# Ends of an attention and FFN trunk on one core: where norm weights load, how the last products are cut, who multiplies last

## The chip, the cores and the metric

The kernel runs on one core of one Trainium2 chip. The metric is the device time of one execution in microseconds (us); less is better. The kernel before was timed three times, with a median of 1301.2 us.

## The reference

Two decoder layers on 512 tokens of width 1024, then a last RMSNorm. The first layer mixes with stick-breaking and native sparse attention, the second with forgetting attention; each ends with a gated MLP that has a causal depthwise convolution on one branch. Cut to what the change touches:

```python
def rmsnorm(x, g):
    x32 = x.astype(jnp.float32)
    y = x32 * lax.rsqrt(jnp.mean(x32 * x32, axis=-1, keepdims=True) + NORM_EPS)
    return y.astype(x.dtype) * g

def conv_glu_ffn(h, w_in, conv_w, conv_b, w_out):
    a, b = jnp.split(h @ w_in, 2, axis=-1)
    a = conv(a, conv_w) + conv_b              # causal, depthwise, width 3
    return (jax.nn.silu(a) * b) @ w_out

def reference(x, ...):
    for layer in range(DEPTH):                # 2
        h = rmsnorm(x, attn_norm[layer])
        x = x + mixer(h)                      # even or odd layer
        x = x + conv_glu_ffn(rmsnorm(x, ffn_norm[layer]), ...)
    return rmsnorm(x, final_norm)
```

## The kernel before

Everything is kept transposed: the residual x is eight chunks X[0] to X[7] of 128 channels (partitions) by 512 tokens, two chunks to a tile. A product with a weight matrix is made in float32 accuracy from three products of rounded halves: high weight by high input, low weight by high input, high weight by low input. So each input chunk is held as a pair (xh, xl, made by scale_x), and each weight block, 128x1024 numbers for eight chunks, is loaded as wraw on the SP queue, cast to whi on ScalarE (L193) and subtracted to wlo on VectorE (L194). wraw, whi and wlo have two buffers each. The norm weights g are folded into xh and xl (tile ng); the division by the root of the mean square is made later, on the results, with the vector rstd. The mean square needs the sum of the squares of all eight chunks (ACC, by squares), a product with ones on TensorE (norm_stats), and inv_sqrt: one step on VectorE, two on ScalarE (logarithm and exponential), three on VectorE.

Work for TensorE is written as generators. unit is one block of 24 products of 512 columns into one PSUM bank, with a use that evacuates it; vgroup makes the values in four token blocks (tb 0 to 3); proj is an output projection that adds into X[m]. A queue, Fill, runs them in order and starts the next one (its weight load) when its predecessor begins: `_start(2)`. In the attention stages pipeline interleaves them with the attention of head pairs.

A scheduler of the framework puts the instructions of each engine into a fixed order, mostly that of the program, with an eye to when operands will be ready. Each engine then runs its list in order; the order rows below show that list.

Start of the program (layer0). The SP queue loads the first weight block in four pieces, then six of the eight x chunks, further weights and constants. The ScalarE queue loads x chunks 0 and 2, and then ng (L569). TensorE runs eight products of zeros (warm) to be busy before there is work. The constant mask32 takes one of the two buffers that the squares use, and maskb is made from it on GpSimd (L166); the third square (chunk 2) waits for that. Four units follow in the queue (here U0, U4, U1, U5: blocks 0, 4, 1, 5 of the first input projection), then a vgroup. Only `_start(2)` is called ahead of the squares, so U1's cast and subtraction stand behind the norm's first step in the lists.

Start of layer 1. The queue holds unit U[0] and a vgroup. U[0] and the token blocks of the vgroup take the two "mm" banks of PSUM in turn; U[0]'s bank is free when q is evacuated (L335), for which rstd must be there.

End of the program (ffn with final, then finish). Eleven blocks of the last projection (GH, GL) make each X[m]. Chunks 0 to 6 go through proj: 33 products of 512 columns, an addition to X[m] (L476), a square on ScalarE, a sum on GpSimd (L239), and a multiplication of X[m] with its norm weight on ScalarE (L931). The last chunk, m = 7, goes through finish, in two token parts of 320 and 192 columns: its 33 products for each part (a call of products), square (addition L291, square L293), the product with ones, and out, which runs inv_sqrt, multiplies all chunks by rstd and stores them with four DMAs. Of the eight multiplications of a part, VectorE makes four (L301) and the one of chunk 7 with its norm weight (L302), GpSimd makes three (chunks 1, 3, 5). The program calls out(0) before square(1).

Of the kernel before, what the change touches and what calls it, by code (L numbers as in the profile page):

```python
# [9 lines left out]
F32 = mybir.dt.float32  # L10
F32R = mybir.dt.float32r
BF = mybir.dt.bfloat16
AF = mybir.ActivationFunctionType
ALU = mybir.AluOpType
# [3 lines left out]
P = 128  # L18
# [86 lines left out]
def trunk(ctx, tc, A):  # L105
# [62 lines left out]
    def warm():  # L168

        z = cp.tile([P, SEQ], BF, name="zero")  # L170
        pool.memset(z, 0.0)
        ps = pp.tile([P, SEQ], F32, tag="t", bufs=1, name="t")
        for n in range(8):
            mm(ps, z[:, 0:P], z, n == 0, n == 7)
# [91 lines left out]
    def finish(srcs, oh, ol):  # L266

        n = len(oh)
        m = NK - 1
        ws = [weights(src, [P, kn, P]) for src, kn in srcs]  # L270
        hw = [(h[:, k], l[:, k]) for (h, l), (_, kn) in zip(ws, srcs) for k in range(kn)]
        parts = (slice(0, 320), slice(320, SEQ))
        st = s_banks()
        pss, sqs = [], []

        def products(b, ks):
            t = parts[b]
            w = t.stop - t.start
            if b == len(pss):
                pss.append(pp.tile([P, SEQ], F32, tag="mm", bufs=2, name="mm"))  # L280
            ps = pss[b][:, 0:w]
            for k in ks:
                h, l = hw[k]
                mm(ps, h, oh[k][:, t], k == 0, False)
                mm(ps, l, oh[k][:, t], False, False)
                mm(ps, h, ol[k][:, t], False, k == n - 1)

        def square(b):
            t = parts[b]
            w = t.stop - t.start  # L290
            dve.tensor_add(X[m][:, t], X[m][:, t], pss[b][:, 0:w])  # L291
            sq = wp.tile([P, SEQ], F32, tag="sq2", bufs=2, name="sq")
            act.activation(sq[:, 0:w], X[m][:, t], AF.Square)  # L293
            sqs.append(sq[:, 0:w])

        def out(b):
            t = parts[b]
            w = t.stop - t.start
            inv_sqrt(rstd[:, t], st[:, b, 0:w], w)
            for c in (0, 2, 1, 4, 3, 6, 5):  # L300
                (pool if c in (1, 3, 5) else dve).tensor_mul(X[c][:, t], X[c][:, t], rstd[:, t])  # L301
            dve.scalar_tensor_tensor(X[m][:, t], X[m][:, t], ng[:, 4, m:m + 1], rstd[:, t], op0=ALU.mult, op1=ALU.mult)  # L302
            for c in range(0, NK, 2):
# [725 lines left out]
```

## Time and profile before

| what | us |
|---|---|
| timed runs | 1303.6, 1301.2, 1296.93 |
| median | 1301.2 |
| the profiled execution | 1299.13 |
| its span on the core | 1297.4 |
| TensorE busy in it | 1269.5 |
| VectorE, ScalarE, GpSimd busy | 694.5, 557.4, 155.1 |
| bytes moved by DMA | 124.00 MB |

The span is what the views of the trace show, from the first instruction to the end; 1.7 us lie around it. Times of rows count from the span's start. A row of the timeline gives start, duration, engine, line of the program, operation and tiles (written <- read), shape and count, and in brackets how long the engine sat idle before and what released it. Products overlap on TensorE, so a duration is longer than the distance to the next start; the distances are what a stream costs. The granted clock of TensorE is given in full speed: 1.00 is 2.4 GHz and 0.50 is 1.2 GHz.

### The profile page before, as it was taken

The page shows a single profiled execution, that of the slowest core. Times are in us where ns is not written, and L with a number is a line of the kernel's source. Part 1 is how long each engine was busy: PE and PEld are TensorE (multiplying, and loading weights), DVE is VectorE, ACT ScalarE, POOL GpSimd, SP SyncE. Part 2 cuts the span into 40 slices and gives each one's busy share as a digit, 9 for nine tenths or more (in the row PEclk, how much of TensorE's full clock was granted, in tenths as well). Part 3 has the DMA queues.
Part 4 walks back from the last instruction along what each step waited for, and adds up shares of the span by engine and source line. Part 5 has one row for each costly group of instructions (what it writes and reads, how often), then busy time and mean ns, then how long its engine had stood idle before and what let it go on. Part 6 is the DMA issues. An engine that isn't in the chain of part 4 may idle for free.

```text
span 1297.4 us, 16449 instructions
## 1 busy us (share of the span) xinstructions
PE 1269.5 (98%) x6297; PEld 1000.7 (77%) x6297; DVE 694.5 (54%) x1135; ACT 557.4 (43%) x948; POOL 155.1 (12%) x213
## 2 busy tenths in 40 slices
PE   8999999999999999999999999999999999999995
PEld 5876856567888888888887877776788888888884
DVE  7468665538655435555453453344755533555534
ACT  6466465645433223334342554444533322333332
POOL 1000032223000000000111433321200000000012
PEclk9999999999999999999999999999999999999997
DMA  6325201003333233232344453411332233333232
GB/s 216 90 65 151 77 29 43 19 25 123 98 98 94 80 103 113 99 97 78 92 129 144 140 146 100 118 43 57 116 97 97 88 91 113 98 98 98 83 95 83
DMA packets 50640, 124.00 MB, mean 96 GB/s; under 512 B 6321, under 2 KB 15793, under 8 KB 50561
## 3 DMA queue, kind: packets, MB, share of 16 engines
q1 hardware_dynamic: 49040, 121.35, 31.0%
q10 hardware_dynamic: 1520, 1.59, 0.4%
q8 instruction: 50, 0.82, 0.3%
q14 instruction: 30, 0.24, 0.1%
HBM read 119.28 MB, written 2.13 MB: 94 GB/s over the span
## 4 chain that ended last, share of the span: by engine, by line
PE 94%; DVE 3%; DMA 1%; ACT 1%; issue 1%; POOL 0%; DVEq 0%; ACTq 0%
PE mm L115 80%; PE s L115 6%; PE o L115 4%; PE t L412 4%; DMA x<-x 1%; DMA mask<-mask 0%; DVE x L301 0%; DVE e L449 0%; DMA wc<-wcv 0%; DVE acc L239 0%; DVE lt L444 0%; DVE wlo L194 0%; ACT lt L441 0%; ACT whi L193 0%; DVE e L450 0%
## 5 line engine op out<-in xcount | busy, mean ns | idle before, releaser
L115 PE MATMUL mm<-xh,whi 128*128 128x512 f32 x944 | 375.8, 398 | 2.4 <-ACT xh L248 2.1
L193 ACT CAST whi<-wraw 128x1024 fp32r<-128x1024 f32 (+2 forms) x221 | 201.6, 913 | 392.7 <-PE mm L115 373.7
L115 PE MATMUL mm<-xl,whi 128*128 128x512 f32 x944 | 369.4, 391 | 0.1
L115 PE MATMUL mm<-xh,wlo 128*128 128x512 f32 x944 | 368.5, 390 | 0.8 <-DVE wlo L194 0.8
L194 DVE TENSOR_TENSOR wlo<-wraw,whi 128x1024 fp32r<-128x1024 f32 (+2 forms) x221 | 236.8, 1072 | 143.0 <-ACT whi L193 140.1
L115 PEld LDWEIGHTS mm<-xh,whi 128*128 128x128 f32 x944 | 177.8, 188 | 46.8 <-issue 9.1
L115 PEld LDWEIGHTS mm<-xl,whi 128*128 128x128 f32 x944 | 177.6, 188 | 39.0 <-issue 1.0
L115 PEld LDWEIGHTS mm<-xh,wlo 128*128 128x128 f32 x944 | 177.9, 188 | 37.0 <-DVE wlo L194 1.5
L115 PE MATMUL mm<-gh,whi 128*128 128x512 f32 (+2 forms) x363 | 139.3, 384 | 0.0
L115 PE MATMUL mm<-gh,wlo 128*128 128x512 f32 (+2 forms) x363 | 139.1, 383 | 0.0
L115 PE MATMUL mm<-gl,whi 128*128 128x512 f32 (+2 forms) x363 | 139.1, 383 | 0.0
L403 POOL TENSOR_SCALAR e<-e,dn 128x512 f32<-128x512 f32 (+3 forms) x128 | 77.4, 625 | 177.3 <-DVE dn L397 91.4
L390 ACT ACTIVATE e<-e,nm 128x512 f32<-128x512 f32 (+3 forms) x128 | 70.4, 551 | 49.4 <-DVE nm L388 49.4
L413 ACT COPY ph<-t 128x512 f32<-128x512 f32 x100 | 58.2, 582 | 70.3 <-PE t L412 70.2
L237 POOL COPY acc<-sq 128x512 f32<-128x512 f32 x4 | 2.8, 707 | 651.4 <-ACT sq L234 651.4
L769 DVE TENSOR_TENSOR a<-mm,rstd 128x512 f32<-128x512 f32 x44 | 30.4, 692 | 92.1 <-PE mm L115 91.9
L476 DVE TENSOR_TENSOR x<-x,mm 128x512 f32<-128x512 f32 x63 | 43.2, 686 | 67.3 <-PE mm L115 67.0
L115 PEld LDWEIGHTS mm<-gh,wlo 128*128 128x128 f32 x363 | 68.2, 188 | 13.5
L115 PEld LDWEIGHTS mm<-gh,whi 128*128 128x128 f32 x363 | 68.2, 188 | 13.4
L115 PEld LDWEIGHTS mm<-gl,whi 128*128 128x128 f32 x363 | 68.2, 188 | 13.2
L777 DVE TENSOR_TENSOR b<-mm,rstd 128x512 f32<-128x512 f32 x44 | 30.4, 692 | 72.4 <-PE mm L115 72.3
L773 ACT ACTIVATE tt<-tt 128x512 f32<-128x512 f32 x44 | 27.8, 632 | 86.8 <-DVE tt L772 86.8
(160 smaller groups left out, 1603.0 us busy)
## 6 DMA issues: line engine op xcount, KB each, us to landing
wraw<-wfi SPq DMA_DIRECT2D x88, 512.0 KB
wraw<-wu SPq DMA_DIRECT2D x31, 512.0 KB
wraw<-wfo SPq DMA_DIRECT2D x32, 384.0 KB
wraw<-wfo SPq DMA_DIRECT2D x32, 320.0 KB
wraw<-wo SPq DMA_DIRECT2D x32, 256.0 KB
cb<-cd SPq DMA_DIRECT2D x8, 512.0 KB
x<-x SPq DMA_DIRECT2D x14, 256.0 KB
wraw<-wv SPq DMA_DIRECT2D x6, 528.0 KB
```

Of the source, the lines that this page charges most:

```text
L115: pe.matmul(out, l, r, start=st, stop=sp_)
L193: act.copy(h, w)
L194: dve.tensor_sub(l, w, h.bitcast(F32))
L237: eng.tensor_copy(ACC[0], sq)
L390: act.activation(ei, ei, AF.Exp, bias=nm, scale=-1.0, accum_out=dn)
L403: pool.tensor_scalar(ei, ei, self.dn[:, hd, i:i + 1], 1.0, op0=ALU.mult, op1=ALU.mult)
L412: pe.transpose(ps[:, o:o + P], self.e[:, hd, EOFF[i] + j * P:EOFF[i] + j * P + P], ident)
L413: act.copy(self.ph[:, 512 * n:512 * n + 512], ps)
L476: dve.tensor_add(X[m], X[m], ps)
L769: dve.tensor_mul(a, ps, rstd)
L773: silu.append(act.activation(t, t, AF.Silu).ins)
L777: dve.tensor_mul(b, ps, rstd)
```

## The change

Four places are edited. At the start, the load of ng is issued first on the ScalarE queue, ahead of x chunks 0 and 2; warm runs 12 products of zeros in place of 8; and `fl._start(3)` is called ahead of norm_stats, so that U1's weights are loaded, cast and subtracted earlier in the lists. In layer 1, unit U[0] writes to an "s" bank of PSUM in place of an "mm" bank. At the end, finish now takes chunks 6 and 7, both in two token parts; the weights of chunk 6 get tiles of their own (fh, fl); the multiplications are all on VectorE; and the additions of the second part stand in its list ahead of the last multiplications of the first.

```diff
@@ warm
-        for n in range(8):
-            mm(ps, z[:, 0:P], z, n == 0, n == 7)
+        for n in range(12):
+            mm(ps, z[:, 0:P], z, n == 0, n == 11)
@@ finish
-    def finish(srcs, oh, ol):
+    def finish(fp, src, oh, ol):
         n = len(oh)
-        m = NK - 1
-        ws = [weights(src, [P, kn, P]) for src, kn in srcs]
-        hw = [(h[:, k], l[:, k]) for (h, l), (_, kn) in zip(ws, srcs) for k in range(kn)]
+        ms = (NK - 2, NK - 1)
+        hw = {}
+        for m in ms:
+            own = lambda sh: tuple(fp.tile(sh, F32R, tag=f"{t}{sh[1]}", bufs=1, name=t) for t in ("fh", "fl"))
+            ws = [(weights(a, [P, kn, P], own if m == ms[0] else None), kn) for a, kn in src(m)]
+            hw[m] = [(h[:, k], l[:, k]) for (h, l), kn in ws for k in range(kn)]
         parts = (slice(0, 320), slice(320, SEQ))
+        width = (320, 192)
         st = s_banks()
...
+        def square(m, b, ps):
+            t, w = parts[b], width[b]
+            added.append(dve.tensor_add(X[m][:, t], X[m][:, t], ps[:, 0:w]).ins)
+            sq = wp.tile([P, SEQ], F32, tag="sq2", bufs=4, name="sq")
+            act.activation(sq[:, 0:w], X[m][:, t], AF.Square)
+            return sq[:, 0:w]
+
+        def scale(b, cs):
             t = parts[b]
...
-            for c in (0, 2, 1, 4, 3, 6, 5):
-                (pool if c in (1, 3, 5) else dve).tensor_mul(X[c][:, t], X[c][:, t], rstd[:, t])
-            dve.scalar_tensor_tensor(X[m][:, t], X[m][:, t], ng[:, 4, m:m + 1], rstd[:, t], op0=ALU.mult, op1=ALU.mult)
-            for c in range(0, NK, 2):
-                (act if c in (0, 4) else sp).dma_start(A["out"][c:c + 2, :, t].rearrange("c p s -> p c s"), XX[c // 2][:, :, t])
+            for c in cs:
+                if c in ms:
+                    dve.scalar_tensor_tensor(X[c][:, t], X[c][:, t], ng[:, 4, c:c + 1], rstd[:, t], op0=ALU.mult, op1=ALU.mult)
+                else:
+                    dve.tensor_mul(X[c][:, t], X[c][:, t], rstd[:, t])
+                if c % 2 == 1:
+                    (act if c in (1, 5) else sp).dma_start(A["out"][c - 1:c + 1, :, t].rearrange("c p s -> p c s"), XX[c // 2][:, :, t])
...
+        sqs = {}
+        added = []
         for b in range(2):
+            for m in ms:
+                ps = pp.tile([P, SEQ], F32, tag="mm", bufs=2, name="mm")
+                if (m, b) == (ms[0], 1):
+                    products(m, b, ps, range(4))
+                    for m2 in ms:
+                        mm(st[:, 0, 0:320], ones, sqs[m2, 0], False, m2 == ms[1])
+                    inv_sqrt(rstd[:, parts[0]], st[:, 0, 0:320], 320)
+                    products(m, b, ps, range(4, n))
+                else:
+                    products(m, b, ps, range(n))
+                if (m, b) == (ms[1], 1):
+                    scale(0, range(5))
+                sqs[m, b] = square(m, b, ps)
+                if (m, b) == (ms[0], 0):
+                    for b2 in range(2):
+                        mm(st[:, b2, 0:width[b2]], ones, ACC[0][:, parts[b2]], True, False)
+        with tc.issue_after(added[-1]):
+            for m2 in ms:
+                mm(st[:, 1, 0:192], ones, sqs[m2, 1], False, m2 == ms[1])
+            inv_sqrt(rstd[:, parts[1]], st[:, 1, 0:192], 192)
+            scale(0, range(5, NK))
+            scale(1, range(NK))
@@ layer0
             h, l, w = weights(U[0], [P, NK, P], pieces=4)
+            act.dma_start(ng, A["ng"])
             load_x(True)
-            act.dma_start(ng, A["ng"])
...
             fl.step(NK - 1)
+            fl._start(3)
             norm_stats(True)
@@ ffn
-                    fl.add(*[proj(m, src(m), GH, GL, use) for m in range(NK - 1)])
+                    fl.add(*[proj(m, src(m), GH, GL, use) for m in range(NK - 2)])
                     fl.all()
-                    finish(src(NK - 1), GH, GL)
+                    finish(fp, src, GH, GL)
@@ layer1
-            fl.add(unit(U[0], q_use(0)), vgroup(wv(0), 272, v_use(0), (v_l1, None)), unit(U[8], k_use(0)),
+            fl.add(unit(U[0], q_use(0), s_bank), vgroup(wv(0), 272, v_use(0), (v_l1, None)), unit(U[8], k_use(0)),
```

VectorE's list at the start, from the first sum of squares (acc) to the norm's steps (rs_t, rs_u, rstd), in the kernel before. The first wlo is U4's, the two behind rs_t are U1's and U5's:

```order
L237 COPY acc<-sq 128x512
L194 TENSOR_TENSOR wlo<-wraw,whi 128x1024
L239 TENSOR_TENSOR acc<-acc,sq 128x512 x7
L259 TENSOR_SCALAR rs_t<-s 128x512
L194 TENSOR_TENSOR wlo<-wraw,whi 128x1024 x2
```

The same stretch of VectorE's list in the changed kernel:

```order
L237 COPY acc<-sq 128x512
L194 TENSOR_TENSOR wlo<-wraw,whi 128x1024
L239 TENSOR_TENSOR acc<-acc,sq 128x512 x5
L194 TENSOR_TENSOR wlo<-wraw,whi 128x1024
L239 TENSOR_TENSOR acc<-acc,sq 128x512 x2
L259 TENSOR_SCALAR rs_t<-s 128x512
```

U1's subtraction has moved ahead of the norm's first step, and stands between the fifth and the sixth of seven additions; on ScalarE its cast stands likewise ahead of the last two squares.

VectorE's list at the end, in the kernel before: from rstd of the first part to the addition of chunk 7's second part (x_1489, x_1492, x_1495 and x_1498 are the tiles of chunks 0 and 1, 2 and 3, 4 and 5, 6 and 7):

```order
L264 SCALAR_TENSOR_TENSOR rstd<-rs_u,rstd 128x320
L301 TENSOR_TENSOR x_1489<-x_1489,rstd 128x320
L301 TENSOR_TENSOR x_1492<-x_1492,rstd 128x320
L301 TENSOR_TENSOR x_1495<-x_1495,rstd 128x320
L301 TENSOR_TENSOR x_1498<-x_1498,rstd 128x320
L302 SCALAR_TENSOR_TENSOR x_1498<-x_1498,ng,rstd 128x320
L291 TENSOR_TENSOR x_1498<-x_1498,mm 128x192
L259 TENSOR_SCALAR rs_t<-s 128x192
```

The same in the changed kernel, where these tiles are x_1493, x_1496, x_1499 and x_1502:

```order
L264 SCALAR_TENSOR_TENSOR rstd<-rs_u,rstd 128x320
L301 TENSOR_TENSOR x_1493<-x_1493,rstd 128x320 x2
L301 TENSOR_TENSOR x_1496<-x_1496,rstd 128x320 x2
L301 TENSOR_TENSOR x_1499<-x_1499,rstd 128x320
L290 TENSOR_TENSOR x_1502<-x_1502,mm 128x192 x2
L301 TENSOR_TENSOR x_1499<-x_1499,rstd 128x320
L299 SCALAR_TENSOR_TENSOR x_1502<-x_1502,ng,rstd 128x320 x2
L259 TENSOR_SCALAR rs_t<-s 128x192
```

All eight multiplications are now in this list; the two additions of the second part (chunks 6 and 7) stand behind five of them, and three stand behind the additions. Outside the start and the end the lists of all engines are the same in both kernels, but for the PSUM bank of U[0] in layer 1.

## Rows read from the trace of the kernel before

**Rows 1.** The page: busy us, share of the span and instructions by engine.
```profile
PE 1269.5 (98%) x6297; PEld 1000.7 (77%) x6297; DVE 694.5 (54%) x1135; ACT 557.4 (43%) x948; POOL 155.1 (12%) x213
```

**Rows 2.** TensorE's waits: total us, times, longest.
```profile
PE s L115 <- ACT sq L293: 5.9, 1, 5.9
...
PE s L115 <- DVE wlo L194: 1.5, 1, 1.5
...
PE mm L115 <- DVE q L335: 1.2, 1, 1.2
```

**Rows 3.** Timeline, start of the program, all engines, to TensorE's fifth block.
```profile
5.96 2.98 ACT L248 ACTIVATE xh<-x,ng 128x512 fp32r<-128x512 f32 x4 [0.75 <-DMA ng<-ng]
...
13.70 1.23 DVE L194 TENSOR_TENSOR wlo<-wraw,whi 128x1024 fp32r<-128x1024 f32 x1 [0.25 <-ACT whi L193]
13.73 1.66 POOL L166 CAST maskb<-mask 128x512 bf16<-128x512 f32 x1 [11.56 <-DMA mask<-mask]
...
14.98 0.50 PE L115 MATMUL mm<-xh,wlo 128*128 128x512 f32 x1 [0.39 <-DVE wlo L194]
...
16.09 4.67 DVE L239 TENSOR_TENSOR acc<-acc,sq 128x512 f32<-128x512 f32 x6 [0.15 <-ACT sq L234]
...
20.81 1.13 PE L115 MATMUL s<-acc,ones 128*128 128x512 f32 x2 [0.56 <-DVE acc L239]
...
22.01 0.39 PE L115 MATMUL s<-xh,whi 128*128 128x512 f32 x1
...
23.91 0.50 PE L115 MATMUL s<-xh,wlo 128*128 128x512 f32 x1 [1.52 <-DVE wlo L194]
```

**Rows 4.** Stretches at the start: busy by engine, granted clock, DMA share, GB/s.
```profile
6.00:8.00 2.00, 1.22 (x3) 0.79 (x4) 1.21 (x2) 1.89 (x3) 0.00 (x0) 0.87 0.88 301
8.00:10.00 2.00, 2.00 (x6) 1.52 (x6) 1.99 (x4) 1.86 (x5) 0.00 (x0) 0.50 1.00 369
```

**Rows 5.** Timeline, start of layer 1, the vgroup's first two token blocks.
```profile
681.14 0.29 PE L115 MATMUL mm<-whi,xl 128*128 128x272 f32 x1
...
682.65 0.39 PE L115 MATMUL mm<-vhi,xh 128*128 128x272 f32 x1 [1.22 <-DVE q L335]
...
683.58 0.46 ACT L341 ACTIVATE vt<-mm,rtok 128x256 f32<-128x256 f32 x1
```

**Rows 6.** Timeline, end of the program, first products of each piece of chunks 6 and 7.
```profile
1264.55 0.39 PE L115 MATMUL mm<-gh,whi 128*128 128x512 f32 x1
...
1272.03 0.30 PE L115 MATMUL mm<-gh,whi 128*128 128x320 f32 x1
...
1276.86 0.25 PE L115 MATMUL mm<-gh,whi 128*128 128x192 f32 x1
...
1278.18 1.05 PE L115 MATMUL s<-acc,ones 128*128 128x320 f32 x4
1279.06 0.70 PE L115 MATMUL s<-sq,ones 128*128 128x320 f32 x2
```

**Rows 7.** Timeline, end of the program, from rstd of the first part.
```profile
1282.64 0.49 DVE L264 SCALAR_TENSOR_TENSOR rstd<-rs_u,rstd 128x320 f32<-128x320 f32 x1
1283.17 3.68 DVE L301 TENSOR_TENSOR x<-x,rstd 128x320 f32<-128x320 f32 x4
1286.78 0.54 DVE L302 SCALAR_TENSOR_TENSOR x<-x,ng,rstd 128x320 f32<-128x320 f32 x1
1287.24 0.34 DVE L291 TENSOR_TENSOR x<-x,mm 128x192 f32<-128x192 f32 x1
...
1288.03 1.01 PE L115 MATMUL s<-sq,ones 128*128 128x192 f32 x2 [5.95 <-ACT sq L293]
1289.08 0.36 DVE L259 TENSOR_SCALAR rs_t<-s 128x192 f32<-128x192 f32 x1 [1.50 <-PE s L115]
...
1291.50 2.34 DVE L301 TENSOR_TENSOR x<-x,rstd 128x192 f32<-128x192 f32 x4
...
1293.77 0.41 DVE L302 SCALAR_TENSOR_TENSOR x<-x,ng,rstd 128x192 f32<-128x192 f32 x1
```

More of the change, by code (lines that the diff above doesn't have):

```diff
@@ L272, in finish @@
         parts = (slice(0, 320), slice(320, SEQ))
+        width = (320, 192)
         st = s_banks()
-        pss, sqs = [], []
-        def products(b, ks):
-            t = parts[b]
[L278 to L299, printed above, removed]
-            for c in (0, 2, 1, 4, 3, 6, 5):
-                (pool if c in (1, 3, 5) else dve).tensor_mul(X[c][:, t], X[c][:, t], rstd[:, t])
-            dve.scalar_tensor_tensor(X[m][:, t], X[m][:, t], ng[:, 4, m:m + 1], rstd[:, t], op0=ALU.mult, op1=ALU.mult)
-            for c in range(0, NK, 2):
-                (act if c in (0, 4) else sp).dma_start(A["out"][c:c + 2, :, t].rearrange("c p s -> p c s"), XX[c // 2][:, :, t])
@@ L306, in finish, with products @@
-        products(0, range(n))
-        square(0)
-        products(1, range(4))
-        for b in range(2):
-            mm(st[:, b, 0:parts[b].stop - parts[b].start], ones, ACC[0][:, parts[b]], True, False)
-        mm(st[:, 0, 0:320], ones, sqs[0], False, True)
-        products(1, range(4, n))
-        out(0)
-        square(1)
-        mm(st[:, 1, 0:192], ones, sqs[1], False, True)
-        out(1)
+        def products(m, b, ps, ks):
+            for k in ks:
+                h, l = hw[m][k]
+                o, t = ps[:, 0:width[b]], parts[b]
+                mm(o, h, oh[k][:, t], k == 0, False)
+                mm(o, l, oh[k][:, t], False, False)
+                mm(o, h, ol[k][:, t], False, k == n - 1)
```

## The prediction

> **What bounds the kernel now.** TensorE is busy for 98% of the span [rows 1], so I read first its waits [rows 2]: what is not a wait of TensorE, or work after its last product, is hidden. Four waits lie where the change is made: 5.9 us at the very end for a square, 1.5 us at the start for U1's wlo, 1.2 us in layer 1 for q; the fourth is the sum of squares at the start, 0.56 us [rows 3]. Then I read the three places in order of time, to see for each what the waiting instruction's own engine did until then [rows 3 to 7]. Between these places the lists of instructions are the same, so I take a gain at the start to be carried to the end.
>
> **The start.** In the trace the sum of squares is the path: GpSimd gets the mask at 13.73 and frees a buffer of the squares 1.66 us later, the additions run from 16.09 in steps of 0.79 (six end at 20.76), and the product with ones starts at 20.81, which I call S [rows 3]. TensorE was not late for it: U4's second product had to wait until 14.98 for its wlo (13.70 and 1.23 us), and 23 products of 0.227 us (the distance in [rows 6], 7.48 us for 33) end by 20.2.
>
> That decides two edits. ng's load, ahead of the x chunks, lets ScalarE begin earlier than 5.96, where it sat idle 0.75 us for ng, and 12 products of zeros keep TensorE busy until then; the granted clock was 0.87 and 0.50 from 6 to 10 us [rows 3, 4]. Both speed up U0 alone, up to some 1.5 us of it, and behind U0 the product waits for U4's wlo all the same: I cost them at nothing, by cover of that wait. One side effect counts: on the SP queue the second x load waits for the first load of the ScalarE queue to land, which was x chunk 0 and is now the small ng. DMA moved 301 GB/s from 6 to 8 us against 369 after that [rows 4]; if the hole closes, 2 us x 68/369 = 0.4 us are won for all that follows in the queue, the mask among them. The price of the move itself, x chunk 0 issued one load later, is bounded by the 0.75 us that ScalarE waited for ng, and hidden there.
>
> `_start(3)` moves U1's cast ahead of the last two squares on ScalarE and its subtraction between the fifth and sixth addition on VectorE. The addition behind it waits, and behind that the product with ones: 1.23 us [rows 3], and I take 0.15 us for the hand-over and give back 0.2, since the last two squares are then ready (0.70 a step, not 0.79): 1.2 us. So S goes to 20.81 + 1.2 - 0.4 = 21.6. What it buys: before, U1's second product came at 23.91, 3.10 us after S. Now its wlo is there, and what remains is the product with ones and one more product, which took 22.01 - 20.81 = 1.20 us. 3.10 - 1.20 - (1.2 - 0.4) = **1.1 us** won. Bounds: if the mask comes no earlier and TensorE's idle time ahead of S (20.2 to 22.0) brings the clock down as it was from 8 to 10 us [rows 4], some 3 us at half speed cost 1.5 us: 0.7 - 1.5 = -0.8. If the subtraction fits into a gap and S stays early: 1.9 + 0.4 = 2.3.
>
> **Layer 1.** U[0] held one of two "mm" banks until q was evacuated. The last product of the vgroup's first token block began at 681.14, the next block's first at 682.65 [rows 5]; by the columns a product costs 0.227 x 272/512 = 0.12, so the hole is **1.4 us**. With U[0] in an "s" bank the second block starts at once. What is late next: the third block takes the first one's bank, which ScalarE frees at 683.58 + 0.46 = 684.04; the second block, 24 products, would end at 681.26 + 2.9 = 684.2. The cover is 0.15 us; whatever is missing there is lost one to one, so 0.9 is the lower bound. The norm's own "s" bank is another one.
>
> **The end, TensorE.** Chunk 6 starts at 1264.55 [rows 6]. 33 products of 320 columns took 4.83 us (1272.03 to 1276.86), 12 of 192 took 1.32, so 33 take 3.63: together 8.46 against 7.48 in one piece. The cut costs 1.0 us, and the products with ones that are added, 0.5 (part one, by the distance from 1279.06) and 0.3. In the new order: 1264.55 + 4.83 + 0.88 (sum, 1278.18 to 1279.06) + 4.83 + 1.32 + 1.06 + 2.31 + 3.63 = 1283.4 for the last product; before it was 1288.03 - 5.95 = 1282.1 [rows 7].
>
> By the Trainium skill (TensorE: Matmul & The Clock Gate, section "Back-to-back issue gap"), an isolated product of N columns costs N/2.4 + 2.5 ns, 136, 82 and 216 ns for 320, 192 and 512, so that the cut would cost 0.1 us, not 1.0, and the time below would be 1293.8. The rows show 146, 110 and 227 ns for these streams, and I go by them.
>
> **The end, VectorE.** Before, the second part's addition (1287.24) stood behind five multiplications of the first [rows 7], 5.2 us after the last product. Now part one's products with ones end at 1264.55 + 12.92 = 1277.5, 2.1 us earlier than before (1279.6), so its rstd is ready at 1283.13 - 2.1 = 1281.0. The price of a multiplication on VectorE alone isn't in the trace: 3.68/4 = 0.92 us for 320 columns with GpSimd at work beside it, 0.49 for another operation of that shape (L264), and 0.46 from the start of L302 to that of the addition behind it. I take 0.46 (nearest: same tiles, same engine), and 0.33 for 192 columns (0.36 for rs_t, less the same overlap; with GpSimd beside it 2.34/4 = 0.59). Five end at 1283.3, so the addition waits for TensorE, not for them: 1283.6 to 1283.9. Square 0.4, product with ones 0.65 (at full clock; 1.01 in the row, 6 us after the last product): 1285.0. VectorE by then has three multiplications more to do, 1.4 us, to 1285.3: rs_t starts there, 1289.08 before. From rs_t to the first multiplication 2.42 us [rows 7], eight of 0.33 to 1290.4, and from the last one's end to the end of the span 1297.4 - 1294.18 = 3.2, stores: 1293.6, and 1293.2 if a multiplication of 192 costs 0.28. **4.0 us** won. Bounds: 3.2 (stores of both parts meet, product at 1.01, multiplications at 0.36) and 4.6.
>
> **Sum.** 1.1 + 1.4 + 4.0 = 6.5 us. Of the profiled execution's 1299.13 us, 1292.6 remain. That execution was 2.1 us faster than the median of the runs, 1301.2; against the median I get **1294.7 us**.
>
> **Rivals.** (a) The start doesn't pay: S is later than I think or the clock falls behind it. For it: the subtraction stands in the path now, and TensorE idles 1.4 us before S. Against: the wait of 1.5 us was a real one. At -0.8 the sum is 4.6: 1296.6. (b) More than I count: S stays early, the stores overlap better: 2.3 + 1.4 + 4.4 = 8.1, 1293.1. (c) The multiplications are slow by themselves, 0.92 and 0.59 us, and GpSimd was not the cause: five end at 1285.6, additions 1286.2, three more 1289.0, rs_t to the first of eight 1291.4, 4.7 us, 3.2 us: 1299.3, 1.9 lost at the end, so 2.5 - 1.9 = 0.6 won: 1300.6. Against: 0.46 and 0.49 for the same shape. (d) Layer 1 gives nothing, since another wait takes the place (the third block's bank): 1296.1. (e) Slower: U1's cast now stands in ScalarE's list ahead of two squares, so if its weights land late, at W, the squares, the sum and all of TensorE wait: S = W + 1.03 (the cast, 128x1024) + 1.23 + 1.5, W + 3.8. It turns the sum negative from S = 28.1, W = 24.3; landing at 26 gives 1302.9. For it: that load is issued on SP behind a wait for U0's pieces. Against: at 369 GB/s [rows 4] its 512 KB are 1.4 us, and W = 24.3 would be 10 us behind the cast of U4's load, which was done by 13.70 [rows 3].
>
> **How the numbers follow.** Forecast 0.50, (a) 0.20, (b) 0.15, (c) 0.05, (d) 0.06, (e) 0.04. The three runs span 6.7 us, so the range holds the scatter of a median as well: 1290.5 to 1298.5 covers the forecast, (b), (d) and most of (a), and leaves out (c) and (e). A measurement of this kernel can tell about 0.5%, 6.5 us, from no change: the forecast lies on that line. Half of its own chance, nearly all of (b) and a share of (a) where the scatter helps count as faster: 0.47. Within 0.5%: 0.48. Slower: (e) and scatter about (c), 0.05 in all, almost none of it by more than 1%.
>
> **What would show it.** At the start: S near 21.6, U1's second product 1.2 us after it with no wait for wlo; a clock below 1.00 behind S would be (a). In layer 1: no wait of TensorE for q, and none for vt. At the end: last product at the old time less 2.5 plus 1.3, multiplications of 320 columns under 0.5 us each, the addition of chunk 7's second part 0.2 us behind the last product. Steps of 0.9 there would be (c). If all three hold and the time doesn't, the carry through the middle failed: a new wait between 40 and 660 us or between 690 and 1260.

## The result, and the profile after

| | before | after |
|---|---|---|
| median of the timed runs, us | 1298.19 (5 runs, 1296.93 to 1303.6) | 1291.88 (5 runs, 1289.55 to 1291.93) |
| profiled execution, us | 1299.13 | 1291.93 |
| its span, us | 1297.4 | 1290.1 |

The ratio of the means is 0.9934 (95% interval 0.991 to 0.9959): the changed kernel is faster, clear of the noise. It is 6.3 us faster in the medians (0.49%) and 7.2 us in the two profiled executions (0.55%), whose spans differ by 7.3. Whether it is faster by more than the 0.5% that the prediction called the limit of a measurement is not settled, as the interval reaches from 0.41% to 0.9%. The forecast was 1294.7 us, on that line, with "within 0.5%" a little ahead of "faster".

The page of the kernel after, its busy line (engine, us, share of the span, instructions; [rows 1] before):

```profile
PE 1271.2 (99%) x6338; PEld 1002.1 (78%) x6338; DVE 693.7 (54%) x1142; ACT 555.7 (43%) x948; POOL 147.9 (11%) x206
```

The waits of TensorE (line, what it waited for: us in all, times, longest; [rows 2] before):

```profile
PE mm L115 <- DVE wlo L194: 3.7, 3, 2.0
...
PE s L115 <- DVE acc L239: 0.9, 1, 0.9
...
PE s L115 <- ACT sq L292: 0.2, 1, 0.2
```

The 5.9 us at the end are 0.2 now, and the wait for q (1.2) is gone. The longest of the waits for wlo that are left, 2.0 us, lies at 128 us, where the kernel before waited 2.2 us for a load: a place that the change doesn't touch. Another, 1.2 us, is U4's at 15.66 (0.39 before, [rows 3]); TensorE waits for the sum of squares behind it all the same.

The start, timeline of the kernel after (start, duration, engine, line, operation, tiles; [rows 3] before):

```profile
13.91 0.61 POOL L166 CAST maskb<-mask 128x512 bf16<-128x512 f32 x1 [11.75 <-DMA mask<-mask]
13.92 1.68 DVE L194 TENSOR_TENSOR wlo<-wraw,whi 128x1024 fp32r<-128x1024 f32 x1
15.52 3.86 DVE L239 TENSOR_TENSOR acc<-acc,sq 128x512 f32<-128x512 f32 x5
15.66 0.50 PE L115 MATMUL mm<-xh,wlo 128*128 128x512 f32 x1 [1.22 <-DVE wlo L194]
19.43 1.22 DVE L194 TENSOR_TENSOR wlo<-wraw,whi 128x1024 fp32r<-128x1024 f32 x1
20.57 1.48 DVE L239 TENSOR_TENSOR acc<-acc,sq 128x512 f32<-128x512 f32 x2
22.11 1.12 PE L115 MATMUL s<-acc,ones 128*128 128x512 f32 x2 [0.93 <-DVE acc L239]
22.67 0.79 PE L115 MATMUL s<-xh,whi 128*128 128x512 f32 x1
23.30 0.40 PE L115 MATMUL s<-xh,wlo 128*128 128x512 f32 x1
```

U1's second product follows S by 1.19 us with no wait, as forecast, but S is at 22.11 and not at 21.6. That second product came at 23.91 before: 0.61 us won. Yet at the next fixed point, the first block of score products, the kernel after is 1.68 us ahead. The rest is in the list of TensorE: in the kernel before, one score product of that block stood alone, much earlier: between U1 and U5, among the vgroup's first products. Timeline of TensorE in the kernel before:

```profile
30.49 1.12 PE L115 MATMUL s<-k,q 64*128 64x512 f32 x2
31.54 0.39 PE L115 MATMUL mm<-vlo,xh 128*128 128x264 f32 x1
...
48.65 0.69 PE L115 MATMUL s<-k,q 64*128 64x512 f32 x1
...
50.62 0.50 PE L115 MATMUL mm<-xh,whi 128*128 128x512 f32 x1
```

And in the kernel after:

```profile
46.97 1.13 PE L115 MATMUL s<-k,q 64*128 64x512 f32 x4
...
48.95 0.50 PE L115 MATMUL mm<-xh,whi 128*128 128x512 f32 x1
```

The lone product (two records in the trace, x2) takes 1.05 us of the stream (30.49 to 31.54). The block that it left takes 1.97 us (48.65 to 50.62), and the full block of the kernel after 1.98: beside its partner the product costs nothing. The two heads of a pair lie in the two halves of the 128 rows, and each product uses 64. By the Trainium skill (TensorE: Matmul & The Clock Gate, section "The mechanism" of the part on packing small matmuls), products on different rows of the array overlap; the rows above agree.

In layer 1, U[0]'s first product in the kernel before:

```profile
670.73 0.39 PE L115 MATMUL mm<-xh,whi 128*128 128x512 f32 x1
```

And in the kernel after, with the seam between the vgroup's first two token blocks ([rows 5] before) and the first product of chunk 6:

```profile
668.88 0.39 PE L115 MATMUL s<-xh,whi 128*128 128x512 f32 x1
...
679.46 0.29 PE L115 MATMUL mm<-whi,xl 128*128 128x272 f32 x1
679.59 0.29 PE L115 MATMUL mm<-vhi,xh 128*128 128x272 f32 x1
...
1261.42 0.30 PE L115 MATMUL mm<-gh,fh 128*128 128x320 f32 x1
```

The second token block follows the first without a wait for q, and chunk 6 starts at 1261.42 (1264.55, [rows 6]): 1.28 us won between U[0] and chunk 6. The end, timeline of VectorE in the kernel after ([rows 7] before):

```profile
1277.94 2.10 DVE L301 TENSOR_TENSOR x<-x,rstd 128x320 f32<-128x320 f32 x5
...
1280.58 0.35 DVE L290 TENSOR_TENSOR x<-x,mm 128x192 f32<-128x192 f32 x1 [0.28 <-PE mm L115]
...
1282.17 0.35 DVE L259 TENSOR_SCALAR rs_t<-s 128x192 f32<-128x192 f32 x1
...
1284.58 1.70 DVE L301 TENSOR_TENSOR x<-x,rstd 128x192 f32<-128x192 f32 x6
```

TensorE there, the products with ones:

```profile
1280.75 1.23 PE L115 MATMUL s<-sq,ones 128*128 128x192 f32 x4 [0.21 <-ACT sq L292]
```

A multiplication of 320 columns takes 0.42 us (0.92 before), one of 192 takes 0.28 (0.59), and the addition of chunk 7's second part waits 0.28 us for TensorE where it stood behind VectorE's list before. From the start of chunk 6 to the end of the span: 28.68 us, 32.85 before, 4.17 won. The traces add up to the 7.3: 1.68 + 1.28 + 4.17, and 0.17 between 48 and 670 us, where the wait at 128 us is 0.18 shorter.

### The profile page after: what moved, and what is told of

It reads as the page before. It is cut to its first block, busy times and chain, and to the rows that moved or that the text cites. A ratio compares the mean times of both kernels' runs of the same rounds, so it can differ in the third digit from the quotient of the medians.

```text
span 1290.1 us, 16521 instructions
## 1 busy us (share of the span) xinstructions
PE 1271.2 (99%) x6338; PEld 1002.1 (78%) x6338; DVE 693.7 (54%) x1142; ACT 555.7 (43%) x948; POOL 147.9 (11%) x206
## 4 chain that ended last, share of the span: by engine, by line
PE 93%; DVE 3%; ACT 2%; issue 1%; DMA 1%; SPq 0%; DVEq 0%; ACTq 0%
PE mm L115 80%; PE s L115 6%; PE o L115 4%; PE t L425 3%; DVE e L462 1%; DVE wlo L194 0%; ACT whi L193 0%; DMA x<-x 0%; ACT xh L248 0%; DMA wraw<-wu 0%; DVE lt L457 0%; DVE acc L239 0%; ACT lt L454 0%; DVE e L463 0%; DVE e L401 0%
## 5 line engine op out<-in xcount | busy, mean ns | idle before, releaser
L115 PE MATMUL mm<-xl,whi 128*128 128x512 f32 x936 | 365.5, 391 | 0.1
L115 PE MATMUL mm<-gh,whi 128*128 128x512 f32 (+2 forms) x352 | 135.0, 383 | 0.0
L115 PE MATMUL mm<-gl,whi 128*128 128x512 f32 (+2 forms) x352 | 134.8, 383 | 0.0
L115 PE MATMUL mm<-gh,wlo 128*128 128x512 f32 (+2 forms) x352 | 134.8, 383 | 0.0
```

The costliest lines, as they stand in the source:

```text
L115: pe.matmul(out, l, r, start=st, stop=sp_)
```

## The experiments

Four kernels are the kernel before with one part of the change each; they share 25 runs of the kernel before (median 1299.14).

**One call alone.**

```diff
             fl.step(NK - 1)
+            fl._start(3)
             norm_stats(True)
```

> The kernel before with the call of _start(3) alone; ng, the zeros, layer 1 and the end stay as before. My theory: this one line carries the whole gain of the start, by two separate effects. First, U1's weights are ready, so its second product comes 1.2 us after the product with ones (S), at the price of S itself going from 20.81 to about 22.1: 0.6 us. Second, the order of TensorE's list changes: in the kernel before, the first score product of a pair stands alone inside U5 and costs 1.05 us there (30.49 to 31.54), while beside the second one of its pair it is free: 1.05 us. Together 1.7 us at the first block of score products (48.65 before), 1.7 to 1.9 at U[0] of layer 1 (670.73 before). Rival: the gain comes from ng and the zeros (U0's first product 0.53 us earlier, full clock), and _start(3) alone only shifts the wait: 0.6 us or less at 48.65.

Measured: 1296.44 us, ratio 0.9978 (0.9965 to 0.9992). The block of score products comes at 46.38, against 48.65 in the profile of before: 2.3 us. A part of this is the mask, which landed earlier in this execution (maskb at 13.37, not 13.73). The profile of the run with the bank alone, below, which has the start of before, has the mask at 13.36 and its lone score product and the rest of the block at 30.14 and 48.30; against it the call wins 1.92 us. There U1's second product came at 23.58, here at 22.77, so 0.81 is the trade of S against U1's weights, and 1.1 the score product, which stands with its partner again. S moved from 20.48 to 21.57. That is the price of the call in all traces: in the six that have the call, the mask in its old buffer and the clock at 1.00, S comes 7.59 us behind the end of maskb, to 0.01, and in three of the four without the call 6.51 (in the kernel before, where U4's subtraction began ahead of maskb, 5.42). So the single call carries the start.

**ng first and twelve products of zeros alone.**

```diff
-        for n in range(8):
-            mm(ps, z[:, 0:P], z, n == 0, n == 7)
+        for n in range(12):
+            mm(ps, z[:, 0:P], z, n == 0, n == 11)
...
+            act.dma_start(ng, A["ng"])
             load_x(True)
-            act.dma_start(ng, A["ng"])
```

> The kernel before with ng's load first and 12 products of zeros, nothing else. My theory: U0 starts half a microsecond earlier and at full clock, but U4's second product waits for its wlo until about 15 to 15.7 either way, S stays where the squares put it (20.8 to 21), U1 waits for its wlo as before (1.5 us), and the score product still stands alone inside U5: 0 us at 48.65 and at 670.73, within 0.3; slower by up to 0.7 if U4's subtraction meets the making of maskb as it did in the changed kernel (1.68 us where it took 1.23). Rival: a gain of about 1 us at 48.65.

Measured: 1298.87 us, ratio 0.9992 (0.9981 to 1.0003). Timeline of TensorE:

```profile
20.71 1.13 PE L115 MATMUL s<-acc,ones 128*128 128x512 f32 x2
...
23.82 0.50 PE L115 MATMUL s<-xh,wlo 128*128 128x512 f32 x1 [1.52 <-DVE wlo L194]
```

S and the wait behind it are those of before, and the score block comes at 48.59. These two edits are worth nothing, as costed. DMA did move more from 6 to 8 us (395 GB/s; 405 in the changed kernel, 301 before, [rows 4]), but what hangs on the mask gained nothing: maskb began at 13.22 here and at 13.17 to 14.55 in the six traces of the changed kernel and its variants that leave the mask in its old buffer, against 13.73, 13.36, 13.37 and 14.06 in the four with the old order. The scatter is wider than the 0.4 us that the prediction took from it.

**The bank alone.**

```diff
-            fl.add(unit(U[0], q_use(0)), vgroup(...
+            fl.add(unit(U[0], q_use(0), s_bank), vgroup(...
```

> The kernel before with U[0] of layer 1 in an s bank and nothing else. My theory: nothing before 670.7 moves, the wait for q (1.22 us) goes, and chunk 6 starts 1.3 us earlier than 1264.55, with the end as it was: 1.3 us in all. Rival: part of it is given back by another wait between 690 and 1260 us, so under 1.0 at chunk 6.

Measured: 1295.89 us, ratio 0.9971 (0.996 to 0.9982), 3.25 us in the medians. In the trace U[0] starts at 668.30 and chunk 6, by its part of 7.48 us ahead of chunk 7's 1268.28, at 1260.80: 592.50 us, 593.82 before, 1.32 won, and nothing given back on the way. In the eight traces with this edit and the old order in inv_sqrt the stretch takes 592.34 to 592.66 us. The median shows more than that, for which the wait itself is a reason (below, the clock).

**The end alone.**

```diff
... the new finish, as above
-                    fl.add(*[proj(m, src(m), GH, GL, use) for m in range(NK - 1)])
+                    fl.add(*[proj(m, src(m), GH, GL, use) for m in range(NK - 2)])
                     fl.all()
-                    finish(src(NK - 1), GH, GL)
+                    finish(fp, src, GH, GL)
```

> The kernel before with the new finish alone (two chunks in two parts, multiplications on VectorE, additions ahead of the last multiplications). My theory: nothing before 1264.55 moves, and from the start of chunk 6 to the end of the span 28.7 us go by where it was 32.85: 4.1 to 4.2 us, the same as in the whole change, so the parts add up. Rival: the end depends on what came before it (weights of chunk 6 and 7 loaded earlier or later): under 3.5 us.

Measured: 1294.89 us, ratio 0.9966 (0.9953 to 0.9979). Chunk 6 starts at 1265.58 and the span ends at 1294.3: 28.7 us, 4.1 won, as in the whole. In these stretches the parts add up: 1.92, 1.32 and 4.13 make 7.4. The differences of the medians don't: 2.7, 0.3, 3.2 and 4.2 make 10.4, and the whole is 6.3 to 7.3. What the clock does in each execution can lie between (below); that it is the whole of the difference was not shown.

**GpSimd multiplies again** (the changed kernel, chunks 1, 3 and 5 on GpSimd).

```diff
-                    dve.tensor_mul(X[c][:, t], X[c][:, t], rstd[:, t])
+                    (pool if c in (1, 3, 5) else dve).tensor_mul(X[c][:, t], X[c][:, t], rstd[:, t])
```

> The changed kernel, but the multiplications of chunks 1, 3 and 5 go back to GpSimd; order, cut and start stay. My theory: beside GpSimd the multiplications of VectorE go back to 0.9 us (320 columns) and 0.58 us (192) from 0.42 and 0.28; the first addition of the second part waits for three of them, to about 1280.7 by the clock of the changed kernel's trace (1279.95 there), and the last eight multiplications take 0.3 us longer. From the start of chunk 6 to the end of the span 29.2 to 29.6 us (28.68 in the changed kernel). Rival: the multiplications of before were slow because of something else (two input tiles being stored, the wait for rstd), so handing three of eight to GpSimd saves VectorE 1.2 us in the first part and 0.9 in the second: 27.8 to 28.2 us.

Measured: one run, 1290.59 us; chunk 6 starts at 1258.80 and the span ends at 1288.8: 30.0 us, 1.3 more than 28.68 and more than my 29.2 to 29.6. Timeline of VectorE, GpSimd and ScalarE:

```profile
1275.32 2.65 DVE L301 TENSOR_TENSOR x<-x,rstd 128x320 f32<-128x320 f32 x3
1275.36 3.32 POOL L301 TENSOR_TENSOR x<-x,rstd 128x320 f32<-128x320 f32 x3 [12.50 <-DVE rstd L264]
...
1277.89 0.60 DVE L290 TENSOR_TENSOR x<-x,mm 128x192 f32<-128x192 f32 x2
...
1279.16 0.61 ACT L292 ACTIVATE sq<-x 128x192 f32<-128x192 f32 x2 [5.52 <-POOL x L301]
```

Three multiplications on VectorE take 2.65 us, five took 2.10 alone. By the Trainium skill (SBUF — State Buffer, section "Who interferes with whom") a VectorE instruction with two inputs in SBUF contends with a GpSimd instruction that reads SBUF; 0.88 us against 0.42 agrees. The term I missed: on ScalarE the squares of the second part stand behind a store that waits for GpSimd's multiplication, so they begin 0.67 us behind the end of the addition (1278.49 to 1279.16); in the changed kernel the second of them began 0.03 us behind its addition. That GpSimd was slow was not the whole price of using it.

**The additions behind all multiplications** (the changed kernel).

```diff
-                    scale(0, range(5))
+                    scale(0, range(NK))
...
-            scale(0, range(5, NK))
```

> The changed kernel, but all eight multiplications of the first part stand ahead of chunk 7's second addition in VectorE's list. My theory: eight multiplications end at about 1281.4 by the clock of the changed kernel's trace, the two additions behind them at 1282.1 (1280.9 in the changed kernel), and rs_t, which there waited behind three multiplications, gives back 0.3: from the start of chunk 6 to the end of the span 29.5 us (28.68). So the order is worth 0.8 us of the 4.2, and the rest is the earlier first part and the faster multiplications. Rival: the order alone is what won the end, as the addition of before stood 5.2 us behind the last product: 31 us or more.

Measured: one run, 1291.69 us. Chunk 6 starts at 1260.31, the span ends at 1289.9: 29.6 us, as expected. The place of the additions in VectorE's list is worth 0.9 of the 4.2 us, and the multiplications without GpSimd 1.3 (the run before). The other 2 us or so are left for the part that no run takes back by itself, chunk 6 cut in two, which lets the first part's rstd come earlier: that share is argued by subtraction, and assumes that the shares add.

**The mask in a buffer of its own** (the changed kernel).

```diff
-    mask32 = wp.tile([P, 2, 2, P], F32, tag="sq", bufs=2, name="mask32")
+    mask32 = wp.tile([P, 2, 2, P], F32, tag="sq2", bufs=4, name="mask32")
```

> The changed kernel, but mask32 lies in a buffer of the last stage (tag sq2) and not in one of the two that the squares use, so that no square waits for the mask. My theory: the mask and maskb decide S. Without them the squares run from 12.3, the additions from about 13.9 with two subtractions of weights between them, and S comes at 21.1 to 21.3 (22.11), just behind U4's last product (21.02): 0.8 to 1.0 us won at the first block of score products (46.97). Rival: the squares are bound by ScalarE and VectorE themselves, the mask being only the last of several equals: under 0.3 us.

Measured: 1289.70 us, ratio 0.9922 (0.9896 to 0.9948), the same 7 runs of before (1299.67) as for the next kernel. S comes at 21.37 and the score block at 46.45, 0.5 us ahead of the changed kernel's first profile and 0.06 ahead of its second (46.51, with S at 21.66). Most of that is when the mask landed. Timeline of this kernel:

```profile
12.89 1.08 POOL L166 CAST maskb<-mask 128x512 bf16<-128x512 f32 x1 [10.72 <-DMA mask<-mask]
...
13.61 0.91 DVE L239 TENSOR_TENSOR acc<-acc,sq 128x512 f32<-128x512 f32 x1
```

S is 7.40 us behind the end of maskb here (13.97), and 7.40 in the last kernel below, which has this edit too; it is 7.59 in the changed kernel. So the buffer is worth 0.2 us, the rival's "under 0.3", and not the 0.8 to 1.0 of my theory: freed of the buffer, the sum still meets the mask, since the addition beside maskb takes 0.91 us where the later ones take 0.69.

**The load at 128 us in another buffer** (the changed kernel).

```diff
-                    wc = spare(1, [P, 16, 64], "wc")
+                    wc = spare(1 if key == "k" else 0, [P, 16, 64], "wc")
```

> The changed kernel, but the weights wc of the second compression are loaded to another of the four spare buffers, which is free earlier than the one that the first compression reads. The wait of TensorE at 128.28 (2.04 us) is behind that load. After it the granted clock was 0.70, 0.50, 0.95 from 128 to 134 in the traces of before, of the changed kernel and of the run with ng and zeros alone, where the wait was 2.0 to 2.2 us, and 1.00 in the runs with the bank alone and the end alone, where it was 1.5 to 1.7. My theory: the wait shrinks to 0.5 us or less and the clock never falls there: 1.6 to 2.0 us won at 192 us against executions without the fall, 3.2 against those with it, and the scatter between executions shrinks by that 1.5 us. Rival: the next thing is late there (the gt additions on VectorE, 126.3, or a subtraction of weights, 128.2): 0 to 0.3 us, and the fall stays.

Measured: 1291.46 us, ratio 0.9935 (0.9912 to 0.9958). Timeline of TensorE, the products that waited:

```profile
125.75 0.95 PE L115 MATMUL mm<-wc,gt 128*62 128x64 f32 x13 [0.47 <-DVE gt L636]
```

The same view, later:

```profile
143.74 0.39 PE L115 MATMUL mm<-vhi,xh 128*128 128x264 f32 x1 [1.76 <-DVE k L346]
```

The wait shrinks from 2.04 to 0.47 us and the clock stays at 1.00, but a wait for k of 1.76 us appears 18 us later: nothing won. TensorE's list changed here too. In the changed kernel a score block stands whole ahead of the compression (its first row: 124.30, x4); here one product of it stands there alone, and the rest comes behind the compression. Timeline of TensorE:

```profile
124.15 1.12 PE L115 MATMUL s<-k,q 64*128 64x512 f32 x2
...
129.29 0.69 PE L115 MATMUL s<-k,q 64*128 64x512 f32 x1
...
131.27 0.51 PE L115 MATMUL mm<-xh,whi 128*128 128x512 f32 x1
```

The block still takes 1.98 us, so the lone product costs about 1 us on top, and the block's results come 5 us later. I expected a rival here, but not in that place; whether the wait for k follows from the new order was not tested by itself.

**The last four** ran side by side, with 9 runs of the kernel before (median 1297.8). First the changed kernel itself.

> The changed kernel itself, beside the three kernels that follow. My theory: its executions come in groups some 1.5 us apart, by whether the granted clock falls behind a wait of TensorE (from 128 to 134 us above all); median between 1289.5 and 1292, spread about 2 us or more. Rival: the groups come from the DMA at the start (the mask lands earlier or later), and the clock falls in every execution or in none.

Measured: 1290.54 us (1289.62 to 1291.28), ratio 0.9939 (0.9926 to 0.9951). There are no two clean groups; the clock fell at 128 us in the profiled one. Chunk 6 to the end takes 28.7 us, as in the first profile.

**The wait at 128 us filled.**

```diff
... Z holds warm's tile of zeros
                 ps2 = pp.tile([P, SEQ], F32, tag="mm", bufs=2, name="mm")
+                if key == "v":
+                    for n in range(8):
+                        mm(ps2, Z[0][:, 0:P], Z[0], n == 0, n == 7)
```

> The changed kernel, but 8 products of zeros stand ahead of the products of the second compression, in the same bank, which those then overwrite. They change no result and bring nothing forward: the load of wc lands when it did. By the distance of the zeros at the program's start they take 1.7 us, so of the wait of 2.04 us ahead of 128.28 some 0.3 us remain, in which TensorE is idle. My theory: the clock falls because TensorE waits there, so with the wait filled it stays at 1.00 from 128 to 134 and the execution is as fast as the fastest of the changed kernel (1289.6), with the group 1.5 us above it gone or rare. Rival: the fall has to do with the many small products of the compression or with the load, not with the idle time: it is still there in about half the executions, and the kernel is slower by what the zeros add, up to 1.7 us.

Measured: 1293.53 us, ratio 0.9964 (0.995 to 0.9977): 3.0 slower than the changed kernel. Windows of the changed kernel in its first profile (stretch, length, busy us and instructions by engine, and then the granted clock, the share of DMA and GB/s):

```profile
128.00:130.00 2.00, 1.72 (x21) 1.75 (x22) 1.38 (x3) 0.79 (x1) 0.00 (x0) 0.70 0.07 15
130.00:132.00 2.00, 2.00 (x16) 1.78 (x15) 2.00 (x6) 0.20 (x1) 0.52 (x1) 0.50 0.00 0
```

The same windows of this kernel:

```profile
128.00:130.00 2.00, 2.00 (x34) 1.93 (x33) 0.23 (x1) 0.00 (x0) 0.00 (x0) 1.00 0.06 11
130.00:132.00 2.00, 2.00 (x11) 1.09 (x11) 1.65 (x5) 0.21 (x1) 0.53 (x1) 1.00 0.02 4
```

The half that concerns the clock agrees, but isn't shown: with TensorE busy ahead of the compression the clock stays at 1.00 here and in the last kernel below, and the small products that ran at half speed before run at full speed; but it also stayed there in five of the seven traces with the call and the wait unfilled, and the mean clock of the timed runs (0.996 to 0.998) is no higher than the changed kernel's beside it (0.996 to 0.999). The time didn't follow, and the spread (1.95 us) isn't smaller. The zeros changed the order of the list: a score product stands alone again, and the wait for k is back, as in the run with the load in another buffer. Timeline of TensorE:

```profile
126.28 1.12 PE L115 MATMUL s<-k,q 64*128 64x512 f32 x2
127.33 0.50 PE L115 MATMUL mm<-xh,whi 128*128 128x512 f32 x1
...
131.06 0.69 PE L115 MATMUL s<-k,q 64*128 64x512 f32 x1
...
133.04 0.50 PE L115 MATMUL mm<-xh,whi 128*128 128x512 f32 x1
```

And later in it:

```profile
145.52 0.39 PE L115 MATMUL mm<-vhi,xh 128*128 128x264 f32 x1 [1.77 <-DVE k L349]
```

1.05 us alone, and the block that it left takes 1.98: the same two numbers, within 0.01, as at the start of the kernel before, in another kernel and another place.

**The mask in its own buffer and the logarithm first** (the changed kernel).

```diff
... mask32, as above
-        dve.tensor_scalar(t, ss, 1.0 / D, EPS, op0=ALU.mult, op1=ALU.add)
         act.activation(u, ss, AF.Ln, bias=eps, scale=1.0 / D)
+        dve.tensor_scalar(t, ss, 1.0 / D, EPS, op0=ALU.mult, op1=ALU.add)
```

> The changed kernel with two edits: mask32 in its own buffer, and in inv_sqrt the logarithm on ScalarE called ahead of the first step on VectorE (rs_t), which in the traces so far came first and held ScalarE up (rs_u waited for rs_t: 1282.17 to 1282.56 at the end). My theory: 0.5 us at the first block of score products, as in the run with the mask alone (46.97 to 46.45), and at the end 0.4 us for the logarithm that no longer waits plus up to 0.3 since rs_t no longer stands behind three multiplications on the path: from the start of chunk 6 to the end 28.0 to 28.3 us (28.68). Together 0.9 to 1.2 us. Rival: both steps read the same bank of PSUM and one waits for the other whichever is first, so rs_t is late instead and the third step waits for it: 0 at the end.

Measured: 1288.31 us (1287.73 to 1290.34), ratio 0.9926 (0.9913 to 0.9938): 2.2 us below the changed kernel beside it, and the best of all. The intervals of the two against the kernel before still overlap. Chunk 6 starts at 1259.27 and the span ends at 1287.5: 28.2 us, 0.45 won. The other half of the forecast missed in this trace: the score block comes at 47.57, 1.06 behind the changed kernel beside it, as the clock fell to 0.50 at 16.1 us and TensorE itself was late (S at 23.08). What makes up for it lies between, where the clock did not fall at 128 us, and in layer 1, which I had not counted: from U[0] to chunk 6 591.91 us, and 591.92 in the next kernel, against 592.34 to 592.66 in the eight traces with the bank and the old order, so the order wins 0.4 to 0.7 us there too. Timeline of ScalarE at the end:

```profile
1279.92 0.42 ACT L259 ACTIVATE rs_u<-s,eps 128x192 f32<-128x192 f32 x1 [0.74 <-PE s L115]
```

And of VectorE:

```profile
1280.38 0.36 DVE L260 TENSOR_SCALAR rs_t<-s 128x192 f32<-128x192 f32 x1 [0.27 <-ACT rs_u L259]
```

The rival was half right: the two readers of the bank still follow one another, but now the one that waits is not on the path.

**All three** (those two edits and the filled wait).

> The changed kernel with the mask in its own buffer, the logarithm first, and the wait ahead of the second compression filled with 8 products of zeros. My theory: the gains add, 0.9 to 1.2 us and the fall of the clock: median about 1288.4 to 1288.8, and a narrower spread than the changed kernel. Rival: the earlier mask makes the wait at the second compression longer or the zeros come late: no better than the mask and the order alone.

Measured: 1291.53 us, ratio 0.9949 (0.9937 to 0.9962). It has the wait for k at 145.12 (1.77 us) and a lone score product at 125.89, like the kernel with the filled wait; from chunk 6 to the end it takes 28.2 us, so the logarithm's gain is there, but the gains don't add.

## Why the prediction was wrong, step by step

**The step that failed** is in the first part: "Between these places the lists of instructions are the same". They are not up to 49 us, and the section on the change is wrong there in the same way; from there to chunk 6 TensorE's list is the same but for U[0]'s bank. The added call moved one score product 18 us down TensorE's list, back to its partner, and that alone is 1.05 us, a term that the sum put at nothing. The order of the two kernels could be read beforehand; the term was left out because I compared the lists where TensorE waits, and a product that runs alone on half of the rows shows no wait. With it, the sum would have been 7.5 us, 0.58% of 1301.2 and on the side of "faster". How little lay between the two is part of the account: 6.5 us were 0.50%, and the chances stood at 0.48 to 0.47. In the two profiles the sum was 0.8 us short: the missing 1.05 and the 0.17 at 128 us, less the half microsecond by which the start term was too large. That 6.5 is so near the 6.3 of the medians is luck, since the medians of the kernel before moved by more than that difference from set to set.

**The start term, 1.1 us,** measured 0.61 in the first pair of traces and 0.81 at the same time of the mask. The 0.4 us for the closed hole of the DMA was wrong: the hole closed and the mask came no earlier; without it the same sum gives 0.7. The rise of S by U1's subtraction (1.2 us forecast) was 1.1 (20.48 to 21.57). The rest of S's rise to 22.11 is the later mask of that execution (its end at 14.52, and 13.98 in the run with the call alone). The clock stayed at 1.00 behind S: of rival (a) the later S held, and the clock didn't. ng and the zeros at nothing: right.

**Layer 1, 1.4 us:** 1.28 and 1.32. Right; nothing else became late there.

**The end, 4.0 us:** 4.17 and 4.13. The last product was forecast 18.85 us behind the start of chunk 6 (1283.4 - 1264.55), and came 18.85 behind it (1280.27); rs_t 20.75 forecast, 20.75 measured. The second is exact by luck: the additions came 0.1 later than forecast and the three multiplications behind them took 0.1 less. So the cut did cost the 1.0 us of TensorE that the rows gave, and the multiplications alone cost 0.42 and 0.28, near the 0.46 and 0.33 that were taken from the same tiles. Rival (c) fell: with GpSimd back they are 0.88 again. The estimate of 0.1 us for the cut, from the gap that the Trainium skill (TensorE: Matmul & The Clock Gate, section "Back-to-back issue gap") gives for an isolated product, would have put the last product 0.9 earlier; the trace of these streams doesn't agree.

**The base.** The forecast of 1294.7 was made against 1301.2, the median of the three runs at hand; the later sets of the same kernel had medians of 1298.19, 1299.14, 1299.67 and 1297.8. So of the 2.8 us between forecast and result between 1.5 and 3.4 are this, and they are no error of the mechanism; against the profiled execution the sum gave 1292.6, and 1291.93 was measured.

## What to carry to other kernels

An edit at one place can reorder a list far behind it: compare the whole list of the engine that bounds, and look for small products that have lost the partner beside which they were free, since no wait shows that. Of a helper engine count not only what it slows by its port but also who stands in a queue behind its result: the squares behind the store were 0.67 of the 1.3 us that GpSimd cost. A median of three runs is a poor base for a change of half a per cent; the stretches between fixed points of a trace added up to 0.1 us, with the start taken at the same time of the mask, where the medians did not add up to 3.

## What the runs showed of the hardware

**The clock behind short waits.** The granted clock went from 1.00 (2.4 GHz) to 0.50 (1.2 GHz) for some 3 us behind a wait of TensorE, or at its end, in some executions and not in others. At 128 to 130 us it did so in four of the 14 profiled executions, behind waits of 2.0 to 2.2 us, and not in the other ten, in one of which the wait was 1.99 us. At the wait for q in layer 1 (1.22 us) it did so in two of the four profiles that have that wait (0.72, 0.50, 0.93 from 678 to 684 us in the run with the call alone; 0.50, 0.65 from 682 in the run with the end alone), and in none of the ten without it. Early in the program, from full clock, it fell in three, behind waits for wlo: at 16.1 and 16.6 us (waits of 1.31 and 1.20 us), and at 26.6, 2.3 us behind one of 1.51; similar waits at the same places left it at 1.00 in other executions. The stretch in layer 1 with its fall (the granted clock is the third number from the end), in the run with the call alone:

```profile
678.00:680.00 2.00, 1.25 (x6) 1.25 (x7) 1.51 (x7) 0.92 (x4) 0.00 (x0) 0.72 0.28 115
680.00:682.00 2.00, 2.00 (x11) 2.00 (x11) 0.17 (x1) 0.45 (x3) 0.00 (x0) 0.50 0.00 0
```

Each fall costs about 1.5 us. From U[0] of layer 1 to chunk 6, with the same products in the same order and the same wait, the two executions without it take 593.82 and 593.83 us, the two with it 595.51 and 595.24. At 128 us the price is alike: in the changed kernel the stretch from the score block to the product at 190 us takes 143.37 us with it, in the kernel with the mask's own buffer 141.58 without it, and the wait was 0.22 longer in the first. So taking a wait away can win more than the wait: the bank alone takes 592.50, 1.3 us less than an execution without the fall and 2.7 to 3.0 less than one with it, which agrees with the 3.2 us in the medians.

A timed run has no trace, but its mean granted clock is on record, and in the 41 runs of the kernel before in the three sets the time goes with it: five runs with a mean of 0.990 took 1301.55 to 1303.11 us, thirteen with 0.995 took 1296.95 to 1298.11. Of the 25 runs beside the bank alone 11 have a mean of 0.992 or less, of its own seven none. So the scatter of some 5 us goes with how often the clock falls, by an estimate from 1.5 us a fall some three times between the fastest and the slowest (a rough one, as the start and the end of a run weigh on the mean as well); at which waits it fell in those runs was not shown.

**Who starts first.** Where U4's subtraction on VectorE and the making of maskb on GpSimd met, the one that began first took its own time and the other paid: wlo at 13.70 took 1.23 us and maskb at 13.73 took 1.66 [rows 3]; with maskb at 13.91 and wlo at 13.92 they took 0.61 and 1.68, and so, within 0.02, in the runs with the call, the bank and the end alone. By the Trainium skill (SBUF — State Buffer, section "Who interferes with whom") the shared port goes to whichever of the two issues first, for the whole instruction; these rows agree to 0.15 us (1.20 left of wlo and 0.61 alone make 1.81 for maskb, 1.66 measured).
